# Opening attention's pools with the last projection unit, and moving key tiles and weight measures

## The chip, the cores and the metric

One core of a Trainium2 chip runs the whole kernel. The metric is the device time of one execution in microseconds (us); lower is better. The core has a matrix engine (PE, with its weight loads PEld), three elementwise engines (DVE, ACT and POOL) and SP, which here only issues DMAs. Each engine takes its instructions in the order in which they were written into its queue, and waits at one whose inputs or buffers are not ready.

## The reference

One inference step of a decoder with two layers, for a prompt of 2048 tokens and for 32 tokens of samples (8 sequences of 4). Every matrix product in the kernel is computed from two f16 halves, high and low, in three products.

```python
def even_mixer(h, w_in, b_fox, lb, hgrn_gain, w_out, hgrn_s0, fox_attend):
    proj = h @ w_in
    qa, fa, ia, ga, qb, kb, vb, gb, fb = _split(proj, ...)
    o_a, s_a = gated_linear_chunked(ha(qa), ha(1.0 - f), ha(ia), ha(jnp.log(f)), hgrn_s0)
    ...
    o_b = fox_attend(hb(qb), kb_h, vb_h, log_fb).reshape(bsz, L, B_WIDTH) * jax.nn.silu(gb)
    out = jnp.concatenate([o_a, o_b], axis=-1) @ w_out

def block(args):                                  # of fox_prompt: 128 queries, 4 heads
    logits = einsum('bthd,bshd->bhts', qi, k) * scale + ci[..., None] - c[:, :, None, :]
    logits = jnp.where(t[:, None] >= key_pos[None, :], logits, -jnp.inf)
    p = jax.nn.softmax(logits, axis=-1)
    return jnp.einsum('bhts,bshd->bthd', p, v)
```

`fox_sample` is the same attention for the sample's 32 tokens against 2048 cached tokens per sequence, gathered from pages, plus the new ones. Layer 1 (`odd_mixer`) is a gated linear attention with its own projections. Each layer adds its output to the residual.

## The kernel before, in words

The program has three stages. The **even phase** multiplies the normalized tokens by the input weights of layer 0 in 32 units, 16 for each half of the prompt (`staged`, `dense`): `v0 g0 qf0 qf1 Bq0 Bg0 v1 g1 qf2 qf3 Bq1 Bg1 Bk0 Bv0 Bk1 Bv1`. Unit 31 is `Bv1` of the second half, the last value projection of attention; its products are `pt_Bv110`, `112`, `114` and `116`, which DVE takes out of PSUM into `Bv` and `Bvs`. Beside the units run smaller jobs. `ahead` loads cached keys for the sample's attention (`kp`), turns them on DVE (L1526, four transposes for one entry of `KEYS`) and multiplies them (`ks`); `KEYS` lists the steps, four to a unit, at which this is done. `beside` loads weights of later units and measures their largest values on DVE (L302, four reductions to a weight); `LATER` lists the units in which a load starts, and the measure follows one unit later. A weight's measure is needed only when that weight is split, in a later stage.

The **attention phase** (`phase_fox`) opens its pools when the even phase's have closed, so that it cannot start beside unit 31. It then draws from two generators: `fox_prompt` (for each head h and each group G of 512 queries, four blocks of scores and then the group's values) and `fox_sample`. `until(self.prompt, FOX_P, sample, FOX_S)` draws from whichever is behind by the ratio 270000 to 500000, where each generator yields its own count of ns of PE time, and ends with the sample. Counting the yields gives 233,267 for the prompt and 395,600 for the sample. So the prompt stands at 213,624 when the sample ends, and 19,643 are left.

A score block is a chain: products `s` (PE), maximum `mx` with the bias `cb`/`cm` (DVE, L1412), exponential (ACT, L1420), scale (POOL, L1428). Its values are a second chain: transposes `pt` (PE, L1448), high half `th` (ACT, L1455), low half `tl` (DVE, L1456), products `fo` (PE), result `fy` (DVE, L1471), store (POOL's queue, L1473). The blocks of the first groups are short, those of G=3 long. The PSUM tag `s` has two banks, `t` two, and `kt` two, which the values use as well once the sample is done (`alone`). The sample begins with `past`, which issues a gather and a burst of constants on POOL and goes on to DVE and PE.

The **odd phase** begins with the output projection of layer 0 (`pt_o`). Its first inputs come from `prepare()`: it splits the weight `w_o000` (halves on ACT, DVE L356, POOL L359 and L363) and the first two pieces of attention's output, `yr0000` and `yr000256`, 256 tokens each (ACT, DVE L1854, POOL L1847 and L1851). Before the change `prepare()` is drawn beside what is left of the prompt: `mux(self.prompt, REST_P, prepare(), REST_S)`, L2131. A piece is split in four steps of two input tiles k: k=0 and 4 on ACT (high) and DVE (low); k=2 and 6 (`YPOOL`) are scaled by POOL (L1847), then high on ACT, low on POOL (L1851). Of the weight, parts 0 and 2 go over POOL, 1 and 3 over ACT and DVE. `pt_o0000` needs 24 products for each 128 tokens, three for each k from 0 to 7. The tag `yr` has two buffers; `wr_o000` and `yr0000` take them, and `yr000256` and `yr000512` follow in them.

The schedule is fixed when the program is built. Several scheduler rules (`issue_after`, priorities) move single instructions ahead of their place, so the order on each engine is shown below where it matters.

Of the kernel before, what the change touches and what calls it, by code (L numbers as in the profile page):

```python
# [19 lines left out]
P = 128  # L20
# [18 lines left out]
EWR = 4  # L39
# [10 lines left out]
KEYS = (*range(4 * 13, 4 * 17, 4), *range(4 * 17, 4 * 31, 2))  # L50
LATER = (*range(4, 14), *range(17, 27))
# [4 lines left out]
FOX_P = 270000.0  # L56
LIN3_A = 40000.0
# [66 lines left out]
class Kern:  # L124
# [1221 lines left out]

    def phase_fox(self):
        tc, nc = self.tc, self.nc
        self.fox = ExitStack()
        f1, f0 = (self.fox.enter_context(tc.tile_pool(name=x, bufs=2, reuse_waits="tile")) for x in ("fe", "fx"))  # L1350
        pp1, pp0 = (self.fox.enter_context(tc.tile_pool(name=x, bufs=2, space=PSUM, reuse_waits="tile"))
                    for x in ("fpa", "fpb"))
        if True:
            fx = Pool(f0, {"P": 20},
                      Pool(f1, {"caus": 1, "q2": 3, "k2": 6, "cb": 2, "st1": 12, "cm": 2, "th": 4, "tl": 4, "y": 1, "v2": 6, "sg": 3}))
            pps = Pool(pp0, {"t": 2, "o": 1, "kt": 2}, Pool(pp1, {"s": 2, "sc": 1}))
            caus = fx.tile([P, P], F32, tag="caus", name="caus")
            nc.gpsimd.memset(caus, 0.0)
            nc.gpsimd.affine_select(caus, caus, [[-1, P]], ALU.is_ge, FAR, base=0, channel_multiplier=1)
            with tc.tile_pool(name="fs", bufs=1, side="right", reuse_waits="tile") as s0:  # L1360
                fs = Pool(s0, {"pg": PG, "kt": 2})
                self.prompt = self.fox_prompt(fx, pps, caus)
                drain(until(self.prompt, FOX_P, self.fox_sample(fs, pps), FOX_S))
# [898 lines left out]
```

## Time and profile before

| | |
|---|---|
| time, median of 3 runs (lowest to highest) | 2288.54 us (2284.19 to 2293.45) |
| the profiled execution: time / span | 2291.65 us / 2289.9 us |
| busy share of the span: PE, DVE, ACT, POOL | 96%, 61%, 43%, 32% |
| granted PE clock, mean | 0.99 |
| unit 31 | 887.8 to 911.4 us |
| attention phase | 911.4 to 1239.0 us |

All times inside the trace count from the start of the span. An idle time stands at the instruction that ended it, with the engine, tile and line that released it. PE is busy nearly all the time, so what counts is where it is not, and what it waited for there.

### The profile page before, as it was taken

The page shows a single profiled execution, that of the slowest core. Times are in us where ns is not written, and L with a number is a line of the kernel's source. Part 1 is how long each engine was busy: PE and PEld are TensorE (multiplying, and loading weights), DVE is VectorE, ACT ScalarE, POOL GpSimd, SP SyncE. Part 2 cuts the span into 40 slices and gives each one's busy share as a digit, 9 for nine tenths or more (in the row PEclk, how much of TensorE's full clock was granted, in tenths as well). Part 3 has the DMA queues.
Part 4 walks back from the last instruction along what each step waited for, and adds up shares of the span by engine and source line. Part 5 has one row for each costly group of instructions (what it writes and reads, how often), then busy time and mean ns, then how long its engine had stood idle before and what let it go on. Part 6 is the DMA issues. An engine that isn't in the chain of part 4 may idle for free.

```text
span 2289.9 us, 58071 instructions
## 1 busy us (share of the span) xinstructions
PE 2195.9 (96%) x23316; PEld 1569.0 (69%) x23316; DVE 1400.7 (61%) x3154; ACT 994.3 (43%) x2216; POOL 724.9 (32%) x787
## 2 busy tenths in 40 slices
PE   7999999999999999899999999999999999999998
PEld 5667667774575588455457888677677667567887
DVE  7767677735564466877776454366665655557454
ACT  5434434321221221566667353554644644555243
POOL 2233234100110111544445354154442422232232
PEclk9999999999999999999999999999999999999999
DMA  7444545796575475977735779324325421115554
GB/s 235 144 124 150 160 150 185 233 238 151 159 184 138 118 204 149 280 223 246 223 111 170 260 219 253 101 71 144 92 97 101 120 79 59 54 52 179 171 179 152
DMA packets 361984, 364.02 MB, mean 159 GB/s; under 512 B 108161, under 2 KB 305090, under 8 KB 357490
## 3 DMA queue, kind: packets, MB, share of 16 engines
q1 hardware_dynamic: 359570, 353.69, 52.7%
q0 software_dynamic: 2144, 6.62, 0.8%
q8 instruction: 183, 3.00, 0.6%
q14 instruction: 87, 0.71, 0.1%
HBM read 245.85 MB, written 97.47 MB: 150 GB/s over the span
## 4 chain that ended last, share of the span: by engine, by line
PE 42%; DVE 3%; ACT 2%; DMA 2%; POOL 2%; issue 1%; SPq 0%; POOLq 0%; DVEq 0%; ACTq 0%
PE pt_o L625 4%; PE pt_o L626 4%; PE pt_o L627 4%; PE pt_Cv L625 2%; PE pt_Cv L627 2%; PE pt_Cv L626 2%; PE o_C L909 1%; PE gl_C L756 1%; PE pt L1448 1%; POOL s_C L842 1%; PE py_C L728 1%; ACT L L1420 1%; DMA wr_o<-in_w_out_odd 1%; PE fo L626 0%; PE fo L627 0%
## 5 line engine op out<-in xcount | busy, mean ns | idle before, releaser
L625 PE MATMUL pt_o<-w_o,act 128*128 128x256 f16 x1024 | 279.4, 273 | 1.4 <-ACT sg1C L682 1.4
L626 PE MATMUL pt_o<-w_o,act 128*128 128x256 f16 x1024 | 279.7, 273 | 0.0
L627 PE MATMUL pt_o<-w_o,act 128*128 128x256 f16 x1024 | 279.3, 273 | 0.0
L625 PEld LDWEIGHTS <-act 128*128 128x128 f16 x2304 | 226.1, 98 | 42.3 <-issue 5.3
L626 PEld LDWEIGHTS <-act 128*128 128x128 f16 x2304 | 226.3, 98 | 31.3 <-issue 2.2
L627 PEld LDWEIGHTS <-act 128*128 128x128 f16 x2304 | 226.1, 98 | 31.4 <-issue 2.6
L789 POOL TENSOR_TENSOR kA<-kA,fA 128x512 f32<-128x512 f32 (+1 forms) x56 | 74.2, 1325 | 367.9 <-PE gl_A L756 307.5
L625 PE MATMUL pt_Cv<-w_Cv,act 128*128 128x256 f16 (+1 forms) x512 | 141.5, 276 | 0.9 <-DVE rh L1959 0.8
L627 PE MATMUL pt_Cv<-w_Cv,act 128*128 128x256 f16 (+1 forms) x512 | 141.4, 276 | 0.0
L626 PE MATMUL pt_Cv<-w_Cv,act 128*128 128x256 f16 (+1 forms) x512 | 141.3, 276 | 0.0
L1420 ACT ACTIVATE L<-L,nm,kc 128x512 f32<-128x512 f32 (+3 forms) x160 | 118.2, 741 | 39.4 <-DVE nm L1418 36.1
L1428 POOL TENSOR_SCALAR L<-L,nm 128x512 f32<-128x512 f32 (+3 forms) x160 | 98.2, 629 | 87.4 <-DVE nm L1424 33.7
L789 POOL TENSOR_TENSOR kC<-kC,fC 128x512 f32<-128x512 f32 (+1 forms) x56 | 81.8, 1461 | 136.6 <-PE gl_C L756 93.1
L1455 ACT ACTIVATE th<-pt 128x512 f16<-128x512 f32 (+3 forms) x159 | 80.9, 526 | 74.1 <-PE pt L1448 73.4
L1526 DVE STREAM_TRANSPOSE kt<-kp 128x512 f32<-128x512 f32 x128 | 82.1, 684 | 40.7 <-DMA kp<-in_cache_fox_k 39.7
L1456 DVE TENSOR_TENSOR tl<-pt,th 128x512 f16<-128x512 f32 (+3 forms) x159 | 94.4, 607 | 16.0 <-ACT th L1455 15.0
L1448 PE MATMUL pt<-ident,L 128*128 128x128 f32 x544 | 89.8, 280 | 9.0 <-DVE tl L1456 5.6
L1448 PEld LDWEIGHTS pt<-ident,L 128*128 128x128 f32 x544 | 65.8, 143 | 39.1 <-DVE tl L1456 10.1
L788 DVE TENSOR_TENSOR qC<-qC,fC 128x512 f32<-128x512 f32 (+1 forms) x56 | 72.9, 1302 | 21.1 <-PE gl_C L756 21.1
L1950 ACT ACTIVATE vC<-pt_Cv,kc 128x512 f32<-128x512 f32 (+1 forms) x40 | 23.9, 598 | 134.0 <-PE pt_Cv L627 134.0
L625 PE MATMUL pt_Bv<-w_Bv,act 128*128 128x260 f16 (+1 forms) x256 | 70.8, 277 | 3.9 <-DVE Bvs L1070 3.9
L363 POOL TENSOR_TENSOR w_o<-wr_o,w_o 128x512 f16<-128x512 f32 x32 | 46.5, 1467 | 79.1 <-ACT w_o L362 55.2
(959 smaller groups left out, 6460.4 us busy)
## 6 DMA issues: line engine op xcount, KB each, us to landing
kp<-in_cache_fox_k SPq DMA_DIRECT2D x128, 256.0 KB, 4.9
pgcache_fox_v<-in_cache_fox_v SPq DMA_DIRECT2D x128, 256.0 KB, 4.1
yr<-yT SPq DMA_DIRECT2D x16, 1024.0 KB, 7.0
x1d<-xo SPq DMA_DIRECT2D x44, 256.0 KB, 4.1
wr_o<-in_w_out_even SPq DMA_DIRECT2D x32, 256.0 KB, 5.5
xo<-in_x_prompt SPq DMA_DIRECT2D x32, 256.0 KB, 4.5
wr_Cv<-in_w_in_odd SPq DMA_DIRECT2D x32, 256.0 KB, 3.4
x1r<-x1d SPq DMA_DIRECT2D x16, 512.0 KB, 4.5
```

The source lines that it names most:

```text
L363: nc.gpsimd.tensor_tensor(lo, r, hi, ALU.subtract)
L625: nc.tensor.matmul(ps, lh[0], rh[0], start=first, stop=False)
L626: nc.tensor.matmul(ps, lh[0], rh[1], start=False, stop=False)
L627: return nc.tensor.matmul(ps, lh[1], rh[0], start=False, stop=last)
L788: nc.vector.tensor_tensor(xv[:, :, 1], xv[:, :, 1], t0.to_broadcast([P, nb, w]), ALU.mult)
L789: nc.gpsimd.tensor_tensor(kv[:, :, 0], kv[:, :, 0], t1.to_broadcast([P, nb, w]), ALU.mult)
L1420: self.last_exp = nc.scalar.activation(lt[:, :w], lt[:, :w], AF.Exp, bias=nm[:, 0:1], scale=ib, accum_out=nm[:, 2 + j : 3 + j])
L1428: nc.gpsimd.tensor_scalar(lt[:, :w], lt[:, :w], nm[:, 1:2], 2.0**14, ALU.mult, ALU.mult)
L1448: nc.tensor.transpose(pt[:, w : w + P], rows[b][s // 4][0][:, (s % 4) * P : (s % 4 + 1) * P], self.ident)
L1455: nc.scalar.activation(th[:, a:w], pt[:, a:w], AF.Copy),
L1456: nc.vector.tensor_tensor(tl[:, a:w], pt[:, a:w], th[:, a:w], ALU.subtract)))
L1526: return self.nc.vector.transpose(kt[:, :, 32 * x : 32 * x + 32], t[:, x].rearrange("p (a e) -> p a e", e=32))
```

## The change

The pools of attention are opened when all of the even phase's pools but the weights, the activations and three PSUM banks have closed, and `until(self.prompt, FOX_A, last, 21120.0)` draws 14000 of the prompt among unit 31's products. `phase_fox` opens the remaining PSUM pool (`kt`, `sc`) and goes on from there. `KEYS` puts two entries into units 13 and 14 in place of one, and ends one unit earlier, so that no key tiles are turned beside unit 31. `LATER` leaves out units 12 and 13 and adds 27 and 28. The sample yields 18000 more after POOL's constants, before DVE and PE use them, so that its count is 413,600 in place of 395,600. In the odd phase nothing is edited.

```diff
-KEYS = (*range(4 * 13, 4 * 17, 4), *range(4 * 17, 4 * 31, 2))
-LATER = (*range(4, 14), *range(17, 27))
+KEYS = (*range(4 * 13, 4 * 15, 2), 4 * 15, 4 * 16, *range(4 * 17, 4 * 30, 2))
+LATER = (*range(4, 12), *range(17, 29))
+FOX_A = 14000.0
...
         with pool("act", side="right") as ap, pool("w", side="right") as w0, pool("wl", side="right") as wp1, \
-                pool("wk") as wp0, pool("nrm") as n0, pool("stt") as sp, pool("ps", space=PSUM) as pp0:
-            wpool = self.wpool = Pool(w0, {"w": 3, "wr": EWR, "rm": 3, "pow": 3, "lr": 1})
+                pool("pj", space=PSUM, side="right") as pp1:
+            inner = ExitStack()
+            wk, wp0, n0, sp = (inner.enter_context(pool(x)) for x in ("wr", "wk", "nrm", "stt"))
+            pp0 = inner.enter_context(pool("ps", space=PSUM))
+            wpool = self.wpool = Pool(w0, {"w": 3}, Pool(wk, {"wr": EWR, "rm": 3, "pow": 3, "lr": 1}))
...
-            pps = Pool(pp0, {"pj": 3, "gr": 2, "st": 1, "o": 2})
+            pps = Pool(pp0, {"gr": 2, "st": 1, "o": 2}, Pool(pp1, {"pj": 3}))
...
                 last = dense(15, 16)
-            drain(last)
-            for t in range(4 * 32, 4 * 32 + 2):
-                self.ahead(wpool, pps, t)
+            inner.close()
+            self.fox_open()
+            drain(until(self.prompt, FOX_A, last, 21120.0))
...
+    def fox_open(self):
+        nc = self.nc
+        self.fox = ExitStack()
+        f1, f0 = self.fox_pool("fe"), self.fox_pool("fx")
...
+        self.more_banks = Pool(None, {"kt": 2, "sc": 1})
+        self.fox_banks = Pool(self.fox_pool("fpa", space=PSUM), {"t": 2, "o": 1, "s": 2}, self.more_banks)
...
+        self.prompt = self.fox_prompt(fx, self.fox_banks, caus)
+
     def phase_fox(self):
...
+        self.more_banks.pool = self.fox_pool("fpb", space=PSUM)
+        with self.tc.tile_pool(name="fs", bufs=1, side="right", reuse_waits="tile") as s0:
+            fs = Pool(s0, {"pg": PG, "kt": 2})
+            drain(until(self.prompt, FOX_P, self.fox_sample(fs, self.fox_banks), FOX_S))
...
+            yield 18000
             tots = one([P, NH], "tots")
             nc.vector.reduce_sum(tots, lfp.rearrange("p s h -> p h s"), axis=mybir.AxisListType.X)
```

Line numbers after the change are 1 higher up to the even phase, and 8 or 9 higher from attention on (L1448 becomes L1456, L1851 becomes L1860).

PE, at the border of unit 31 and attention. Tiles `s000`, `s010` are scores of head 0, group 0, blocks 0 and 1; `pt0000` is the first transposed block; `pt_Bv112` to `116` belong to unit 31. Before:

```order
L627 MATMUL pt_Bv116_12572<-w_Bv11_11533,act_121 128x256
...
L625 MATMUL s000_12672<-k2_00_12660,q2_00_12659 128x128
...
L625 MATMUL s010_12695<-k2_00_12660,q2_00_12659 128x256
...
L625 MATMUL s020_12710<-k2_00_12660,q2_00_12659 128x384
...
L625 MATMUL s030_12725<-k2_00_12660,q2_00_12659 128x512
...
L1448 MATMUL pt0000_12770<-ident_58,L000_12676 128x128
```

After:

```order
L626 MATMUL pt_Bv112_12627<-w_Bv11_11658,act_127 128x256
...
L626 MATMUL s000_12434<-k2_00_12422,q2_00_12421 128x128
...
L626 MATMUL s010_12516<-k2_00_12422,q2_00_12421 128x256
...
L627 MATMUL pt_Bv112_12627<-w_Bv11_11658,act_127 128x256
...
L626 MATMUL s020_12531<-k2_00_12422,q2_00_12421 128x384
...
L626 MATMUL s030_12546<-k2_00_12422,q2_00_12421 128x512
...
L1456 MATMUL pt0000_12591<-ident_58,L000_12438 128x128
...
L626 MATMUL s040_12562<-k2_00_12422,q2_01_12504 128x512
...
L627 MATMUL pt_Bv116_12897<-w_Bv11_11658,act_127 128x256
...
L626 MATMUL fo00_12558<-th0000_12596,v2_00_12423 128x512
```

The last product of unit 31 stood ahead of the first score. Now the scores of group 0, most of group 1's and the first values (`fo00`) stand among the products of `pt_Bv112`, `114` and `116`.

SP's DMA queue at the same place. `q2`, `k2`, `v2` and `cb` are attention's loads, `vd1` stores of unit 31's values, `cbd` the store of the bias that `cb0` reads back. Before:

```order
L1325 DMA cbd_80<-cmask_11954 64x128
L1084 DMA vd1_75<-Bvs110_12403 128x2x512
L1084 DMA vd1_75<-Bvs112_12484 128x2x512
L1564 DMA scd_85<-scs15_12429 128x128
L1084 DMA vd1_75<-Bvs114_12545 128x2x512
L1384 DMA q2_00_12659<-qd_71 128x2x512
L1386 DMA_TRANSPOSE k2_00_12660<-kd0_72 128x2x512
L1377 DMA cb0_12664<-cbd_80 128x512
```

After:

```order
L1329 DMA cbd_80<-cmask_12092 64x128
L1392 DMA q2_00_12421<-qd_71 128x2x512
L1394 DMA_TRANSPOSE k2_00_12422<-kd0_72 128x2x512
L1385 DMA cb0_12426<-cbd_80 128x512
L1396 DMA v2_00_12423<-vd0_74 128x4x256
...
L1085 DMA vd1_75<-Bvs110_12490 128x2x512
```

The loads stood behind three stores of `vd1`, each of which waits for a product of unit 31. Now they follow `cbd` at once.

POOL at the end of the prompt. `L315.` are scales of the last score block, `fy320`, `fy330` and `fy332` the last three results, `ys` the sample's; `w_o000`, `yr0000` and `yr000256` are `prepare()`'s. Before:

```order
L359 TENSOR_SCALAR wr_o000_17999<-wr_o000_17999,kc_67 128x512 x2
...
L363 TENSOR_TENSOR w_o000_18006<-wr_o000_17999,w_o000_18006 128x512
L1847 TENSOR_SCALAR yr0000_18004<-yr0000_18004,kc_67 128x512 x2
L363 TENSOR_TENSOR w_o000_18006<-wr_o000_17999,w_o000_18006 128x512
L1428 TENSOR_SCALAR L3150_17968<-L3150_17968,nm315_18032 128x512
...
L1851 TENSOR_TENSOR act_17992<-yr0000_18004,act_17992 128x2x256
...
L1851 TENSOR_TENSOR act_17992<-yr0000_18004,act_17992 128x2x256
L1847 TENSOR_SCALAR yr000256_18126<-yr000256_18126,kc_67 128x512 x2
L1851 TENSOR_TENSOR act_17992<-yr000256_18126,act_17992 128x2x256 x2
L1473 DMA yT0_81<-fy330_18179 128x256
...
L1473 DMA yT0_81<-fy332_18311 128x256
```

After:

```order
L1436 TENSOR_SCALAR L3153_17839<-L3153_17839,nm315_17888 128x512
L1481 DMA yT0_81<-fy320_17915 128x512
L1777 DMA yT0_81<-ys_13859 128x32 x4
L1481 DMA yT0_81<-fy330_18069 128x256
L360 TENSOR_SCALAR wr_o000_18280<-wr_o000_18280,kc_67 128x512 x2
L1481 DMA yT0_81<-fy332_18241 128x256
L364 TENSOR_TENSOR w_o000_18287<-wr_o000_18280,w_o000_18287 128x512 x2
L1856 TENSOR_SCALAR yr0000_18285<-yr0000_18285,kc_67 128x512 x2
L1860 TENSOR_TENSOR act_18279<-yr0000_18285,act_18279 128x2x256 x2
L1856 TENSOR_SCALAR yr000256_18300<-yr000256_18300,kc_67 128x512 x2
L1860 TENSOR_TENSOR act_18279<-yr000256_18300,act_18279 128x2x256 x2
```

Before, all of `prepare()`'s POOL work stood ahead of the store of `fy332`, the prompt's last. Now only the scale of `wr_o000` does; the rest stands behind that store. DVE and ACT have `prepare()`'s work behind the prompt's last `tl` and `th` in the same way.

## Rows read from the trace of the kernel before

**Rows 1.** The page's part 1, busy time and share of each engine.

```profile
PE 2195.9 (96%) x23316; PEld 1569.0 (69%) x23316; DVE 1400.7 (61%) x3154; ACT 994.3 (43%) x2216; POOL 724.9 (32%) x787
```

**Rows 2.** Windows at attention's start: length, then each engine's busy time, PE's clock.

```profile
core 0: us, PE busy (x) PEld busy (x) DVE busy (x) ACT busy (x) POOL busy (x), PEclk, DMA share, GB/s
900.00:910.00 10.00, 10.00 (x116) 8.68 (x115) 5.93 (x11) 1.89 (x4) 1.97 (x4) 1.00 0.32 111
911.40:932.00 20.60, 12.90 (x65) 6.14 (x65) 14.56 (x65) 9.92 (x26) 10.13 (x23) 0.83 1.05 294
932.00:950.00 18.00, 12.75 (x69) 6.89 (x70) 12.82 (x49) 11.62 (x30) 14.58 (x33) 1.00 1.07 326
950.00:960.00 10.00, 9.97 (x86) 6.50 (x85) 9.44 (x37) 6.58 (x18) 4.32 (x7) 1.00 0.78 259
```

**Rows 3.** PE's waits, 905 to 932 us: total us, times, longest.

```profile
PE s L625 <- DVE mx L1412: 3.5, 4, 2.6
PE s L625 <- DVE Bvs L1070: 3.0, 1, 3.0
PE pt L1448 <- POOL L L1428: 1.0, 2, 0.6
```

**Rows 4.** Windows with a lowered clock, columns as above.

```profile
915.00:922.00 7.00, 4.05 (x12) 1.17 (x9) 3.88 (x22) 2.42 (x7) 2.79 (x7) 0.51 1.08 304
1215.50:1225.50 10.00, 8.05 (x32) 5.01 (x33) 6.92 (x16) 6.81 (x16) 7.41 (x8) 0.50 0.36 107
```

**Rows 5.** Timeline of SP's DMA issues around 900 us: start, length, line.

```profile
892.19 0.51 SPq L1325 DMA_DIRECT2D cbd<-cmask  x1
908.63 1.73 SPq L1384 DMA_DIRECT2D q<-qd  x1
910.46 1.28 SPq L1386 DMA_TRANSPOSE k<-kd  x1
```

**Rows 6.** DMA issues, 900 to 950 us: count, size, median us to landing.

```profile
cb<-cbd SPq DMA_DIRECT2D x7, 256.0 KB, 5.1
k<-kd SPq DMA_TRANSPOSE x6, 6.1
```

**Rows 7.** PE's waits, 390 to 430 us.

```profile
PE pt_Bv L625 <- DVE Bvs L1070: 3.9, 3, 1.7
```

**Rows 8.** Timeline of DVE around 410 us, idle before in brackets.

```profile
409.37 0.69 DVE L302 TENSOR_REDUCE rm_Cqk<-lr_Cqk 128x1 f32<-128x512 f32 x1 [1.04 <-DMA lr_Cqk<-in_w_in_odd]
412.99 0.69 DVE L302 TENSOR_REDUCE rm_Cqk<-lr_Cqk 128x1 f32<-128x512 f32 x1 [0.86 <-DMA lr_Cqk<-in_w_in_odd]
```

**Rows 9.** The page's part 5: key tiles turned on DVE.

```profile
L1526 DVE STREAM_TRANSPOSE kt<-kp 128x512 f32<-128x512 f32 x128 | 82.1, 684 | 40.7 <-DMA kp<-in_cache_fox_k 39.7
```

**Rows 10.** Windows at the prompt's end and behind the border.

```profile
1205.00:1225.00 20.00, 15.17 (x74) 8.87 (x73) 15.91 (x42) 15.31 (x34) 17.41 (x19) 0.76 0.18 54
1240.00:1249.50 9.50, 9.50 (x90) 8.49 (x88) 1.25 (x2) 6.16 (x10) 1.71 (x2) 1.00 1.02 341
```

**Rows 11.** Timeline of DVE, 1213 to 1240 us.

```profile
1213.49 1.73 DVE L356 SCALAR_TENSOR_TENSOR w_o<-wr_o,kc,w_o 128x512 f16<-128x512 f32 x1
1216.02 1.84 DVE L1854 SCALAR_TENSOR_TENSOR act<-yr,kc,act 128x512 f16<-128x512 f32 x2
1239.18 0.48 DVE L1471 SCALAR_TENSOR_TENSOR fy<-fo,kc,fsg 128x256 f32<-128x256 f32 x1 [0.94 <-PE fo L627]
```

**Rows 12.** Timeline of POOL, 1227 to 1240 us.

```profile
1227.42 3.69 POOL L1847 TENSOR_SCALAR yr<-yr,kc 128x512 f32<-128x512 f32 x2
1231.09 2.27 POOL L1851 TENSOR_TENSOR act<-yr,act 128x512 f16<-128x512 f32 x2
1239.96 0.55 POOL L1473 DMA_DIRECT2D yT<-fy  x1 [1.01 <-DVE sam_o L665]
```

**Rows 13.** Line L363, whole trace: shortest, median, longest ns.

```profile
L363 POOL TENSOR_TENSOR w_o<-wr_o,w_o x32: 1149/1253/3247, 1213.5 to 2220.3; 128x512 f16<-128x512 f32 x32
```

**Rows 14.** Tile yr, 1175 to 1300 us: from issue to landing.

```profile
DMA to landing us min/median/max: 2.6/6.3/11.6
```

More of the change, by code (lines that the diff above doesn't have):

```diff
@@ L1345, in log_sigmoid @@
         nc.vector.scalar_tensor_tensor(zz, q, -2.0, zz, ALU.mult, ALU.add)
-    def phase_fox(self):
[L1348 to L1363, printed above, removed]
@@ new lines, in fox_pool @@
+    def fox_pool(self, name, **kw):
+        return self.fox.enter_context(self.tc.tile_pool(name=name, bufs=2, reuse_waits="tile", **kw))
+    def fox_open(self):
+        nc = self.nc
+        self.fox = ExitStack()
+        f1, f0 = self.fox_pool("fe"), self.fox_pool("fx")
+        fx = Pool(f0, {"P": 20},
+                  Pool(f1, {"caus": 1, "q2": 3, "k2": 6, "cb": 2, "st1": 12, "cm": 2, "th": 4, "tl": 4, "y": 1, "v2": 6, "sg": 3}))
+        self.more_banks = Pool(None, {"kt": 2, "sc": 1})
+        self.fox_banks = Pool(self.fox_pool("fpa", space=PSUM), {"t": 2, "o": 1, "s": 2}, self.more_banks)
+        caus = fx.tile([P, P], F32, tag="caus", name="caus")
+        nc.gpsimd.memset(caus, 0.0)
+        nc.gpsimd.affine_select(caus, caus, [[-1, P]], ALU.is_ge, FAR, base=0, channel_multiplier=1)
+        self.prompt = self.fox_prompt(fx, self.fox_banks, caus)
```

## The prediction

> **What bounds the kernel now.** I read the page's busy shares first: PE is busy for 96% of the span [rows 1], so 94 us of idle PE is nearly all that a change of order can win, besides stretches at a lowered clock. Then I read the windows around the places that the change touches. Attention's start stands out. In 900 to 910 us, inside unit 31, PE is busy 10.00 of 10 us while DVE is busy 5.93, ACT 1.89 and POOL 1.97; from 911.4 to 932 us PE is busy only 12.90 of 20.60 us, from 932 to 950 us 12.75 of 18.00, and from 950 us it is full again [rows 2]. So 7.70 us are idle in the first stretch and 5.25 us in the second. The waits name the causes: 3.0 us once on DVE's `Bvs` and 3.5 us on the maxima `mx` [rows 3]. The first has a wrong label. DMA issues show that `q` is issued only at 908.63 us and `k` at 910.46 us, while the bias store `cbd` ahead of them went at 892.19 us [rows 5]; the first score waits for `k`, whose loads take a median of 6.1 us in this stretch [rows 6]. The second is a chain: PE, DVE, ACT and POOL pass one short block on, and nothing else is there for PE. Both happen because attention begins when unit 31 has ended. The idle time also costs clock: the granted clock is 0.51 from 915 to 922 us, the lower level of 1.2 GHz, with PE busy for 4.05 us of it [rows 4]; at the upper level the same work takes half, so 2.0 us more are lost.
>
> **Part 1, the early start.** The chance is to hide what lies before 932 us beside a unit that leaves the other engines idle. The listing shows how far the prompt gets among unit 31's products: all scores of group 0, most of group 1's and group 0's values, which is what PE does until about 932 us before. The chance is 7.70 + 2.0 = 9.7 us. Two things come off. First, `q2_00` now follows `cbd`: with `cbd` at 892.2 us, `q` 1.7 us and `k` 1.3 us long at issue [rows 5], `k2_00` is issued at about 894.5 us and landed by 898 to 900.5 us if 3.5 us (estimate, from the idle 3.0 us after the issue at 910.46 us) to 6.1 us pass. PE reaches `s000` after 91 products of unit 31, 887.8 + 91 x 0.106 = 897.5 us, at 0.106 us a product (90 in 9.50 us [rows 10]). That leaves 0.5 to 3 us, of which I take 1, since DMAs are less busy there (share 0.32 at 900 us against 1.05 [rows 2]). Second, the added yield of 18000 keeps the sample back for 0.54 x 18000 = 9.7 us of prompt work, in which the prompt is alone. Alone it lost 5.25 us in 18 us [rows 2], 0.29 us per us, so up to 2.8 us; in 950 to 960 us, with groups that are longer, nearly nothing. I take 1. The 5.25 us after 932 us I leave as they are: they are `mx` chains of group 2 and POOL's constants (POOL busy 14.58 of 18 us), and the change does not take either away. Part 1 gives 9.7 - 1 - 1 = **7.7 us**, bounds 2 and 14 (with all 5.25 us gone).
>
> **Part 2, key tiles and measures.** From 390 to 430 us, PE waits three times, 3.9 us in all, for `Bvs` in unit 13 [rows 7]. Just ahead of it DVE measures `Cqk2`: four reductions of 0.69 us and waits of 1.04 and 0.86 us for their loads [rows 8], 4.6 us in all with DVE waiting at the head of its queue. `LATER` without units 12 and 13 takes these away from here, more than the 3.9 us by which PE is late. They return as 2.7 us of DVE work (the 4 reductions) around units 27 to 29; two entries of `KEYS` in unit 13 and 14 bring eight transposes of 0.684 us [rows 9] where four were, 2.7 us more of DVE. Unit 31 loses its own. Where PE has no wait in these units now, DVE has room for them; in unit 13 it may keep a part of the 3.9 us late. I take **2.5 us** (3.9 less half of 2.7), bounds 0 and 4.
>
> **Part 3, the prompt's end.** Before, `prepare()` stands among the last blocks, and it shows: from 1205 to 1225 us PE is busy 15.17 of 20 us [rows 10], with DVE's `w_o` and `act` splits of 1.73 and 1.84 us ahead of the `tl` that PE waits for [rows 11]. Then the clock is 0.50 for 10 us with 8.05 us of work [rows 4], 4.0 us lost. Together 4.8 + 4.0 = 8.8 us. After the change, the prompt is 14000 ahead and the sample counts 413,600, so the prompt would stand at 14,000 + 0.54 x 413,600 = 237,344 when the sample ends. It has only 233,267. It runs out first, and the listing shows `prepare()` behind it. The splits no longer disturb the last blocks, but the exponentials of the last block still stand in one chain, the values find only two banks (`alone` is false), and the sample's copies now fall among them; I take 5.5 of the 8.8 us back.
>
> The price is at the border. Take T as the end of the last `fo` product. On POOL, the store of `fy332` waits for DVE's `fy` (0.48 us [rows 11]) and takes 0.55 us to issue [rows 12]. Behind it stand two `w_o` low halves of 1.25 us (the median [rows 13]), two scales of `yr0000` (3.69 us) and its two low halves (2.27 us) [rows 12]: T + 0.48 + 0.55 + 2.5 + 3.69 + 2.27 = T + 9.5 us. The products of `pt_o0000` need the first of those low halves at k=2 and the second at k=6. By T + 9.5 us PE can have done 18 products, 18 x 0.106 = 1.9 us. So PE stands 7.6 us where it went on without a gap before. Then `yr000256`: its buffer is that of `wr_o000`, free at about T + 4 us, and a load takes 6.3 us to landing [rows 14]; with 0.7 us on ACT the first product of `pt_o0002`, two products on from there, waits till about T + 11.3 us: 1.6 us more. `yr000512` has the buffer of `yr0000`, free at T + 9.5 us, landed at T + 16 us, some 1.6 us late again. Together 10.8 us, and I add 2 us for the lowered clock behind such a gap, as after 915 us [rows 4]. Border: **-12.8 us**, bounds -5 (if half of it is covered) and -20 (below). Part 3 is 5.5 - 12.8 = -7.3 us.
>
> On POOL's term, a row shows a wide spread: the same `w_o` low half takes 1.149 to 3.247 us [rows 13], and DVE's split at 1213.49 us took 1.73 us, that at 1216.02 us 0.92 us for the same amount [rows 11]. The Trainium skill (GPSIMD Engine Reference, Key points) says why that may be: POOL shares its SBUF interfaces with DVE, and they contend when the DVE instruction has two SBUF inputs, as these splits have. By that rule the border is a bad place, since the change sets DVE's four splits and POOL's six operations side by side; by it the `w_o` term would be 6.5 us in place of 2.5 us and the sum 4 us worse.
>
> **Sum.** 7.7 + 2.5 + 5.5 - 12.8 = +2.9 us won. The profiled execution took 2291.65 us, which becomes 2288.8 us. It lies 3.1 us above the median of the runs, 2288.54 us; from that I predict 2285.6 us. One measurement of this kernel tells from no change what is over 0.5%, 11.4 us.
>
> **Rivals.**
> A, the start gains all and the tail is clean: ahead by 14 us, the prompt meets the sample with long groups, as in 950 to 960 us, so the 5.25 us go too, and all 8.8 us of the tail. 7.70 + 5.25 + 2.0 - 1 + 2.5 + 8.8 - 12.8 = 12.5 us, 2276.0 us. For it: every wait named there is one of short blocks. Against it: DVE was busy 12.82 of 18 us there, and POOL's burst remains.
> B, the border decides, slower: POOL's two halves at 3.25 us (+4.0 us) and the load of `yr000256` at its longest, 11.6 us in place of 6.3 [rows 13, 14]. PE stands 11.6 us to k=6, then to T + 4 + 11.6 + 0.7 = T + 16.3 us, 2.6 us more, and again for `yr000512`, 3 us; with 2.8 us of clock it is 20 us. With a start of 5 us, 1 us from part 2 and 2 us back at the tail, 12 us are lost: 2300.5 us. It decides from a border of 7.7 + 2.5 + 5.5 = 15.7 us on. Against it: the median of that operation is 1.25 us, and 6.3 us that of the loads.
> C, the change only moves the stall: loads and `mx` chains then hold PE inside unit 31, since its queue is in order. `k` at 6.1 us gives 3 us at `s000`, `cb` at 5.1 us [rows 6] another 2 us at `s020`, so that part 1 gives 3 us; 3 + 2.5 + 5.5 - 12.8 = -1.8 us, 2290.3 us.
>
> **How the numbers follow.** Forecast 0.45, A 0.25, B 0.15, C 0.15. A lies just over the bound: two thirds of it are faster by over 0.5%, and one fifth of the forecast's spread, 0.26 in all. Half of B and a tenth of the forecast and C are slower by over 0.5%: 0.13. The rest, 0.61, is within. The range reaches from A with part 2 at its upper bound and the border 3 us cheaper, 2271 us, to just short of B, 2299 us; the forecast's own is 2278 to 2293 us.
>
> **What would show it.** Right: PE with no idle time of over 1 us in unit 31, less than 6 us idle from its end to 40 us later, and a clock of 1.00 there; no wait for `Bvs` in unit 13; at the border an idle of 6 to 9 us before `pt_o0000`, released by POOL's `act` or `yr`, and one of 1 to 2 us released by the load of `yr`. Wrong: a border with under 4 us of idle (A), one over 15 us (B), or idle of over 4 us on `s` inside unit 31 (C).

## Result: 0.42% slower

The changed kernel takes 2297.27 us (median of 18 runs, 2290.00 to 2309.15), the kernel before 2289.01 us beside it (18 runs, 2284.19 to 2299.98). The ratio is 1.0042, 95% interval 1.0030 to 1.0053: 9.6 us lost, where 2.9 us gained were forecast. The time lies inside the predicted range, the sign is wrong.

The page of the changed kernel shows busy times that answer to [rows 1]:

```profile
span 2295.4 us, 58071 instructions
PE 2196.7 (96%) x23316; PEld 1569.3 (68%) x23316; DVE 1401.7 (61%) x3154; ACT 994.9 (43%) x2216; POOL 725.9 (32%) x787
```

PE works as long as before, to 0.8 us. So the loss is idle PE, and the question is where. The profiled execution took 2297.09 us, 5.4 us more than that of before (2291.65 us), so the two profiles show only a part of the 9.6 us. Where a stage starts later than before, the time was lost ahead of it. The starts are those of the first product of each stage in the two timelines (in us; negative is earlier):

| start of | before | after | lost or won since the row above |
|---|---|---|---|
| unit 13 | 392.67 | -4.00 | 4.0 won |
| unit 14 | 430.87 | -4.37 | |
| unit 15 | 454.14 | -1.83 | 2.5 lost |
| unit 16 | 477.44 | +1.30 | 3.1 lost |
| unit 18 | 523.38 | +8.00 | 6.7 lost |
| unit 31, the last even one | 887.78 | +8.89 | 0.9 lost |
| out-projection (`pt_o0000`) | 1238.97 | -0.91 | 9.8 won: unit 31, attention and its tail |
| odd layer's first `Cv` | 1410.79 | +8.26 | 9.2 lost: the border |
| end | | +5.5 | 2.7 won |

Attention and the border together come out near the forecast: one gives about what the other takes. In these two profiles the loss is in the even phase, where 2.5 us were to be gained. PE's waits from 390 to 520 us in the changed kernel (columns: total us, times, longest; [rows 7] has before's, to 430 us):

```profile
PE pt_Bk L626 <- DVE Bvs L1071: 7.4, 1, 7.4
PE ks L1579 <- DVE kt L1534: 6.7, 3, 4.1
PE pt_Av L626 <- DVE Bvs L1071: 0.7, 1, 0.7
```

The waits of `pt_Bv` in unit 13 are gone, as forecast. In their place PE stands once for 7.4 us at unit 14's start, and for 6.7 us at the products of the key tiles. The DMA issues from 400 to 432 us say why. First the kernel before, then the changed one (count, KB each, median us to landing; the last line is for the `vd` stores alone):

```profile
kp<-in_cache_fox_k SPq DMA_DIRECT2D x4, 256.0 KB, 4.1
vd<-Bvs SPq DMA_DIRECT2D x3, 256.0 KB, 3.6
DMA to landing us min/median/max: 2.2/3.6/5.3
```

```profile
kp<-in_cache_fox_k SPq DMA_DIRECT2D x8, 256.0 KB, 5.9
vd<-Bvs SPq DMA_DIRECT2D x4, 256.0 KB, 6.9
DMA to landing us min/median/max: 3.5/6.9/10.0
```

A key tile is four loads of 256 KB, 1 MB. With the second tile of unit 13 in the same stretch, the stores of the unit's values, `vd<-Bvs`, land after a median of 6.9 us in place of 3.6. A buffer of `Bvs` comes free only when its store has landed. The timelines of DVE and SP show one such wait (start, length, operation, idle time before it):

```profile
424.73 0.48 DVE L1064 TENSOR_SCALAR Bv<-pt_Bv,kc 128x256 f32<-128x256 f32 x1 [6.13 <-DMA vd<-Bvs]
```

```profile
411.31 2.79 SPq L1530 DMA_DIRECT2D kp<-in_cache_fox_k  x4
...
414.66 0.39 SPq L1085 DMA_DIRECT2D vd<-Bvs  x1
```

This store is the one that took 10.0 us. It was issued behind the second tile's four loads and a 1 MB store of a weight (`wd`), which the kernel before has there too. DVE stands 6.13 us for it, then empties unit 13's PSUM, and unit 14's first product waits for that. The table hides it: without this wait unit 14 would start some 11.8 us early (an estimate, 4.37 and 7.4; it is 10.4 us in e7, which has no second tile there), not 4.4. Later the loads of the next tiles are late themselves. SP, DVE and PE around 510 us:

```profile
498.70 1.88 SPq L1530 DMA_DIRECT2D kp<-in_cache_fox_k  x4
...
505.23 1.82 SPq L1530 DMA_DIRECT2D kp<-in_cache_fox_k  x4
```

```profile
509.37 2.49 DVE L1534 STREAM_TRANSPOSE kt<-kp 128x512 f32<-128x512 f32 x4 [22.59 <-DMA kp<-in_cache_fox_k]
```

```profile
511.92 1.93 PE L1579 MATMUL ks<-kt,qz 128*32 128x128 f32 x32 [4.05 <-DVE kt L1534]
513.78 0.61 PE L626 MATMUL pf_Ag<-act,w_Ag 128*128 128x512 f16 x1
...
517.99 0.38 PE L627 MATMUL pf_Ag<-act,w_Ag 128*128 128x512 f16 x1
```

The four loads issued from 498.70 us on land after 7.0 to 9.0 us (in e9, below, they were issued from 497.09 us on and landed after 4.7 to 6.8). DVE turns the tile as soon as the last has landed, but that is late (509.37 us; 504.27 us in the kernel before), and PE stands 4.05 us at the head of its queue. After that gap the products run at 0.61 us each where 0.38 us is had at 517.99 us: the granted clock is 0.50 from 512 to 518 us, the lower level of 1.2 GHz.

At attention's start the windows of the changed kernel answer to [rows 2] (unit 31, then the next 20.6 and 18 us; same columns):

```profile
896.70:926.80 30.10, 29.64 (x246) 23.60 (x246) 18.43 (x66) 10.57 (x28) 10.33 (x19) 1.00 0.90 222
926.80:947.40 20.60, 16.53 (x94) 8.75 (x91) 18.55 (x70) 14.40 (x36) 12.65 (x27) 1.00 1.06 335
947.40:965.40 18.00, 14.71 (x92) 9.62 (x92) 12.92 (x41) 11.16 (x31) 13.46 (x26) 1.00 0.82 276
```

Unit 31 carries the prompt's opening groups with 0.46 us idle, and the clock stays at 1.00; 4.07 and 3.29 us are idle behind it, where before it was 7.70 and 5.25 us. The prompt's tail, against [rows 10]:

```profile
1215.00:1225.00 10.00, 8.64 (x74) 6.60 (x74) 6.69 (x13) 4.53 (x11) 3.22 (x5) 1.00 0.07 28
1225.00:1235.00 10.00, 9.38 (x85) 8.21 (x84) 8.87 (x26) 4.42 (x8) 5.79 (x7) 1.00 0.07 21
```

18.02 of 20 us are busy, at full clock. The 20 us of [rows 10] (15.17 us busy) end some 13 us earlier, as seen from the prompt's end. From 1185 us to the prompt's end, 3.43 us are idle in place of 6.15, and the clock, 0.50 for 10 us before [rows 4], stays at 1.00. The border follows, as timelines of PE, DVE and POOL:

```profile
1238.06 0.28 PE L626 MATMUL pt_o<-w_o,act 128*128 128x256 f16 x1 [1.73 <-ACT act L1862]
1238.99 0.27 PE L627 MATMUL pt_o<-w_o,act 128*128 128x256 f16 x1 [0.65 <-POOL w_o L364]
1242.85 0.40 PE L628 MATMUL pt_o<-w_o,act 128*128 128x256 f16 x1 [3.58 <-DVE act L1863]
```

```profile
1236.37 0.48 DVE L1479 SCALAR_TENSOR_TENSOR fy<-fo,kc,fsg 128x256 f32<-128x256 f32 x1 [0.64 <-PE fo L628]
1236.77 4.48 DVE L357 SCALAR_TENSOR_TENSOR w_o<-wr_o,kc,w_o 128x512 f16<-128x512 f32 x2
1241.17 4.73 DVE L1863 SCALAR_TENSOR_TENSOR act<-yr,kc,act 128x512 f16<-128x512 f32 x2
```

```profile
1237.76 2.28 POOL L364 TENSOR_TENSOR w_o<-wr_o,w_o 128x512 f16<-128x512 f32 x2
1240.01 3.11 POOL L1856 TENSOR_SCALAR yr<-yr,kc 128x512 f32<-128x512 f32 x2
1243.09 2.25 POOL L1860 TENSOR_TENSOR act<-yr,act 128x512 f16<-128x512 f32 x2
```

The three gaps are 5.96 us, the largest released by DVE's split of `act`, not by POOL. Behind them the products come 0.21 us apart until 1248.3 us and 0.11 us apart from there on; the granted clock is 0.73 from 1236.3 to 1248 us. The rows give DVE's four splits in pairs; one by one they take 0.74 and 3.82 us (`w_o`) and 1.62 and 3.19 us (`act`). In [rows 11] the `w_o` split took 1.73 us and the two of `act` 0.74 and 1.18 us, although POOL was at work beside these as well.

### The profile page after: what moved, and what is told of

It reads as the page before. It is cut to its first block, busy times and chain, and to the rows that moved or that the text cites. A ratio compares the mean times of both kernels' runs of the same rounds, so it can differ in the third digit from the quotient of the medians.

```text
span 2295.4 us, 58071 instructions
## 1 busy us (share of the span) xinstructions
PE 2196.7 (96%) x23316; PEld 1569.3 (68%) x23316; DVE 1401.7 (61%) x3154; ACT 994.9 (43%) x2216; POOL 725.9 (32%) x787
## 4 chain that ended last, share of the span: by engine, by line
PE 46%; DVE 4%; DMA 3%; POOL 2%; ACT 2%; issue 2%; SPq 1%; POOLq 0%; DVEq 0%; ACTq 0%
PE pt_o L627 4%; PE pt_o L626 4%; PE pt_o L628 4%; PE pt L1456 2%; PE pt_Cv L626 2%; PE pt_Cv L628 2%; PE pt_Cv L627 2%; PE pv L1759 1%; PE o_C L910 1%; PE gl_C L757 1%; PE fo L626 1%; PE fo L627 1%; PE fo L628 1%; PE s L626 1%; PE s L628 1%
## 5 line engine op out<-in xcount | busy, mean ns | idle before, releaser
L1456 PE MATMUL pt<-ident,L 128*128 128x128 f32 x544 | 89.8, 279 | 3.7 <-DVE tl L1464 2.0
L1456 PEld LDWEIGHTS pt<-ident,L 128*128 128x128 f32 x544 | 65.5, 143 | 33.0 <-DVE tl L1464 8.8
L626 PE MATMUL pt_Bk<-w_Bk,act 128*128 128x256 f16 x256 | 70.5, 275 | 7.4 <-DVE Bvs L1071 7.4
L626 PE MATMUL pt_Av<-w_Ai,act 128*128 128x256 f16 x256 | 70.9, 277 | 1.3 <-DVE Bvs L1071 0.7
```

What stands on the lines that cost most here:

```text
L626: nc.tensor.matmul(ps, lh[0], rh[0], start=first, stop=False)
L1456: nc.tensor.transpose(pt[:, w : w + P], rows[b][s // 4][0][:, (s % 4) * P : (s % 4 + 1) * P], self.ident)
```

## The experiments

Each was timed in five rounds beside the kernel before, on the same chip as that. The first theory was that the key tiles cost it: two tiles moved from units 30 and 31 into units 13 and 14, into a stretch full of transfers. Its rivals: the moved measures (`LATER`), the border, or the early start itself. "New `KEYS`" and "new `LATER`" are the lists of the change.

**e1 and e2: one list each, in the kernel before.**

```diff
 e1, from before:
-KEYS = (*range(4 * 13, 4 * 17, 4), *range(4 * 17, 4 * 31, 2))
+KEYS = (*range(4 * 13, 4 * 15, 2), 4 * 15, 4 * 16, *range(4 * 17, 4 * 30, 2))
 e2, from before:
-LATER = (*range(4, 14), *range(17, 27))
+LATER = (*range(4, 12), *range(17, 29))
```

> The kernel before with the new KEYS alone (two key tiles in units 13 and 14, single in 15 and 16, none beside unit 31). Theory 1 (the second key tile loses the time: its 1 MB load stands in the DMA queue ahead of unit 13's store of Bvs, and the loads of the next two tiles come late): slower than before by 6 to 10 us, about 2297 us, with PE waits of several us at the end of unit 13 and on ks in units 15 to 17. Theory 2 (the new place of the weight buffers, wr in an inner pool, delays the loads) and theory 3 (the moved measures of LATER do it): no change, 2289 us within 2 us.

> The kernel before with the new LATER alone (no fetches in units 12 and 13, two more in 27 and 28). Theory 1: 2 to 4 us faster than before, about 2286 us, since the 3.9 us of waits for Bvs in unit 13 go and nothing takes their place. Theory 3 (LATER is what loses the time): 5 us or more slower than before. Theory 2: no change.

e1: 2297.72 us, ratio 1.0032 (1.0020 to 1.0045), 7.3 us lost. e2: 2285.91 us, 0.9976 (0.9963 to 0.9989), 5.5 us won. The two halves of part 2 have opposite signs, and the half that was priced at a loss of 1.35 us of DVE work costs 7.3 us. In e2's profile unit 14 starts 9.7 us early and PE's waits from 390 to 520 us are small:

```profile
PE pt_Bk L625 <- DVE Bvs L1070: 1.0, 1, 1.0
PE pt_Av L625 <- DVE Bvs L1070: 0.7, 1, 0.7
PE ks L1571 <- DVE kt L1526: 0.6, 1, 0.6
```

**e3 and e4: other places for the tiles, other end of the prompt.**

```diff
 e3, from after:
-KEYS = (*range(4 * 13, 4 * 15, 2), 4 * 15, 4 * 16, *range(4 * 17, 4 * 30, 2))
+KEYS = (48, 50, *range(4 * 13, 4 * 17, 4), *range(4 * 17, 4 * 30, 2))
 e4, from after:
-FOX_S = 500000.0
+FOX_S = 560000.0
```

> The changed kernel with another KEYS: two tiles in unit 12, one each in units 13 to 16, then two per unit up to unit 29, so that unit 31 stays free of key work and units 13 and 14 have one tile each as before. Theory 1: 6 to 10 us faster than the changed kernel, 2288 us, about the time of before or below it. Theories 2 and 3: no change from the changed kernel, 2297 us.

> The changed kernel with FOX_S = 560000 in place of 500000, so that the prompt stands at 14,000 + 0.482 x 413,600 = 213,400 when the sample ends, as before the change, and prepare() finds about 20,000 of it to stand beside. Theory A (the border's 9 us come from prepare() being uncovered): the idle PE at the border goes, the disturbed last blocks of before return with up to 8.8 us, so 1 to 5 us faster than the changed kernel, 2292 to 2296 us. Theory B (the border's waits come from the loads and POOL's queue, whatever is drawn beside): no change at the border, 2297 us.

e3 (both extra tiles in unit 12): 2299.05 us, 1.0036 (1.0022 to 1.0050). By the times no better than after. Its unit 14 starts 1.8 us late, where that of after starts 4.4 us early. e4 (the sample lasts longer, so that `prepare()` is covered again): 2298.73 us, 1.0039 (1.0026 to 1.0053). The border's cost falls from 9.2 to 5.7 us, and the stretch from unit 31 to the border wins 6.0 us in place of 9.8: a part of the cost moves into the last blocks, as PE's waits from 1210 to 1265 us show:

```profile
PE fo L626 <- ACT th L1463: 4.8, 2, 3.1
PE pt_o L626 <- ACT w_o L363: 2.9, 1, 2.9
PE fo L627 <- DVE tl L1464: 1.8, 3, 0.7
PE pt_o L627 <- POOL w_o L364: 1.0, 1, 1.0
```

**e5: new `KEYS` in the kernel before, the two extra tiles without their loads.** Their tiles are filled with zeros by POOL, so the sample's key products of these two are left out of the result; all of DVE's and PE's work on them stays.

```diff
 e5, from e1:
                 for x in range(4):
+                    if n in (1, 3):
+                        nc.gpsimd.memset(kp[:, x], 0.0)
+                        continue
                     self.page_load(kp, "cache_fox_k", regs[x], x)
```

> The kernel before with the new KEYS (measured at +7 us), but the second key tiles of units 13 and 14 are filled with zeros on POOL in place of their 1 MB loads; it leaves out these two loads, and everything else of the tiles (turning on DVE, products) stays. Theory load (the second tile's loads crowd the DMA queue there): back to 2289 us within 2 us. Theory DVE (the four more transposes of 0.68 us per unit ahead of the evictions that PE waits for lose the time): stays near 2297 us.

2292.54 us, 1.0001 (0.9988 to 1.0014), against 1.0032 for e1: without 2 MB of loads, the 7.3 us are gone. The stores of `Bvs`, 400 to 432 us, e1 and then e5:

```profile
kp<-in_cache_fox_k SPq DMA_DIRECT2D x8, 256.0 KB, 4.8
vd<-Bvs SPq DMA_DIRECT2D x3, 256.0 KB, 8.1
```

```profile
kp<-in_cache_fox_k SPq DMA_DIRECT2D x4, 256.0 KB, 4.9
vd<-Bvs SPq DMA_DIRECT2D x3, 256.0 KB, 2.6
```

The key loads land as fast in the one as in the other. The medians of the stores are not of the same stores: in e1 only the second of the unit's stores has a landing on record, 8.1 us; the second one in e5 took 5.0 us (5.3 in the kernel before). What costs the time is transfers, not work: that the times show. How much of the 7.3 us goes through this store they do not. e1's profile, of its fastest execution (e5's is of its slowest), has PE waiting 2.3 us at unit 14's start and 2.3 us for key tiles.

**e6: after, with no early start.**

```diff
-FOX_S = 500000.0
+FOX_S = 470000.0
-FOX_A = 14000.0
+FOX_A = 0.0
```

> The changed kernel without the early start: FOX_A = 0, so that the prompt begins behind unit 31 as before, and FOX_S = 470000, so that the prompt runs out at the same place of the sample as in the changed kernel and the border to the next layer stays as it is there. Theory 1 (the early start gains 7 to 10 us): 7 to 10 us slower than the changed kernel, about 2305 us. Rival (the early start gains nothing, its waits only move): as the changed kernel, 2297 us.

2303.74 us, 1.0050 (1.0031 to 1.0069), 1.8 us over after by the ratios (11.4 against 9.6 us), which the intervals do not separate. In the profile the stretch from unit 31 to the out-projection wins 2.8 us here, 9.8 us in after: 7.0 us for the start by this pair, the size of part 1 (7.7 us). Other kernels with the new `KEYS` and no early start scatter in this stretch: 5.2 us won in e1, 5.6 in e9, 1.8 lost in e13, all below. So single profiles give the start some 4 to 12 us.

**e7: after, with two key tiles less.** The last two tiles are not turned at all, so their part of the sample is left out of the result.

```diff
-KEYS = (*range(4 * 13, 4 * 15, 2), 4 * 15, 4 * 16, *range(4 * 17, 4 * 30, 2))
+KEYS = (*range(4 * 13, 4 * 17, 4), *range(4 * 17, 4 * 30, 2))
...
             nc.sync.dma_start(self.scd[:, j * P : (j + 1) * P], self.scs)
+            if j == 14:
+                nc.sync.dma_start(self.scd[:, 15 * P :], self.scs)
```

> The changed kernel with one key tile each in units 13 to 16 and two per unit in 17 to 29: 30 of the 32 tiles; it leaves out the last two tiles of the cached keys. Theory 1 (the two tiles that came from unit 30 cost about 7 us wherever they stand in units 12 to 14): 2290 us. Rival (the new place of the weight buffers or the moved measures lose the time): 2296 us or more.

2284.93 us, 0.9976 (0.9962 to 0.9989). In the changed kernel two key tiles in units 13 and 14 are worth 15 us (0.9976 against 1.0042); their own work on PE is about 2 us of that (the 32 products of one take 1.08 us in e9's trace). Unit 14 starts 10.4 us early, attention wins 9.7 us and the border loses 8.7 us, as in after: the rest of the change is as it was.

**e8: other units left out of `LATER`.**

```diff
 from before:
-LATER = (*range(4, 14), *range(17, 27))
+LATER = (*range(4, 12), *range(17, 24), *range(26, 31))
```

> The kernel before with LATER in units 4 to 11, 17 to 23 and 26 to 30, so that no fetch falls in units 24 and 25, where the new LATER alone showed DVE waiting 5.4 us for a key tile behind a 1 MB fetch and PE 4.9 us behind DVE. Theory (that collision takes back 4 to 5 us): 2 to 5 us faster than the new LATER alone, 2281 to 2284 us. Rival (it only moves to another unit): 2286 us.

2286.58 us, 0.9977 (0.9965 to 0.9989), the same as e2. So these two do not tell where the fetches should go. In e2's profile the moved fetches make a wait of 4.9 us (`gl_A` on DVE's `qA`, 640 to 760 us), which e8's does not have, but e8 has one of 2.9 us (`ks` on `scs`) that e2's lacks and before's shows too.

**e9: both lists in the kernel before.**

```diff
 from before: KEYS as in e1, LATER as in e2
```

> The kernel before with the new KEYS and the new LATER, and nothing else of the change. Alone they measured +7 us and -5.5 us. Theory sum (they add): +2 us, 2292 us. Theory bound (without the measures PE runs ahead in unit 13 until it meets the store of Bvs that the second tile's load delays, so LATER's gain is lost and the key tiles' price shows in full): +8 to +10 us, 2299 us, that is the whole loss of the change, with the early start and the border behind it cancelling each other.

2291.78 us, 1.0010 (0.9994 to 1.0026), 2.3 us lost; e1 and e2 add up to 1.8. So the two lists do not share one bound. With the new `LATER` the tiles cost 7.8 us here (1.0010 against 0.9976 in e2), about as without it, and 15 us in the changed kernel (e7). Beyond the lists, 7.3 us of after's loss (9.6 less 2.3) come with the moved pools, the early start and the yield. Without the tiles these cost nothing that the times show: e7 has the ratio of e2, 0.9976, though it also spares the two tiles' own work. Yet e9 has after's order, instruction for instruction on each engine, up to the last even unit. Its waits from 390 to 520 us:

```profile
PE pt_Bk L625 <- DVE Bvs L1070: 7.4, 1, 7.4
PE ks L1571 <- DVE kt L1526: 2.7, 2, 2.0
```

The same 7.4 us in unit 14, but 4.0 us less on the key tiles. Unit 18 starts 1.25 us late in e9, 8.00 us in after.

**e10, e11 and e12: after, with the pressure lowered.**

```diff
 e10, from after:
-LATER = (*range(4, 12), *range(17, 29))
+LATER = (*range(4, 11), *range(17, 30))
 e11, from e10:
-FOX_S = 500000.0
+FOX_S = 530000.0
 e12, from after:
-KEYS = (*range(4 * 13, 4 * 15, 2), 4 * 15, 4 * 16, *range(4 * 17, 4 * 30, 2))
+KEYS = (*range(4 * 12, 4 * 16, 4), *range(4 * 16, 4 * 30, 2))
```

> The changed kernel with LATER in units 4 to 10 and 17 to 29, so that one more 1 MB fetch leaves the DMA queue ahead of unit 13, where the second key tile's load and the store of Bvs stand. Theory load: the 7.4 us wait at the end of unit 13 shrinks, 3 to 8 us faster than the changed kernel, 2289 to 2294 us. Rival (the wait there belongs to the tile's own 1 MB alone): as the changed kernel, 2297 us.

> The same with FOX_S = 530000, so that some 9,000 of the prompt are left beside prepare() when the sample ends. Theory: half of the border's 9 us come back and less than that is lost in the prompt's last blocks, 2 to 4 us faster than with 500000. Rival (as with 560000, what the border wins the last blocks lose): no difference.

> The changed kernel with key tiles single in units 12 to 15 and two per unit from unit 16 on, 32 in all. Theory load (a second tile costs where the DMA queue carries stores that PE waits for, and unit 16 has fewer of them than unit 13): 4 to 8 us faster than the changed kernel, 2289 to 2293 us. Rival (the two tiles cost about the same wherever they stand, as they did in unit 12): 2297 us.

e10 (one unit's measures less ahead of unit 13): 2289.11 us, 1.0002 (0.9989 to 1.0016). e11: 2287.63 us, 0.9992 (0.9978 to 1.0005), not told from e10. e12 (one tile a unit from unit 12, two from 16): 2290.04 us, 1.0007 (0.9995 to 1.0020). The fetch of one unit's measures, or the place of the double tiles, takes back 8 to 9 of the 9.6 us. The wait at unit 14 falls to 1.4 us in e10, 390 to 520 us:

```profile
PE ks L1579 <- DVE kt L1534: 4.7, 3, 2.2
PE pt_Bv L626 <- DVE Bvs L1071: 2.2, 1, 2.2
PE pt_Bk L626 <- DVE Bvs L1071: 1.4, 1, 1.4
```

**e13, e14 and e15: e10 taken apart.** The theory that was left: the start and the border together are a net loss.

```diff
 e13, from before: KEYS as in e1, LATER as in e10 (pools, start and yield as before)
 e14, from before: LATER as in e10
 e15, from e10:
-            yield 18000
```

> The kernel before with the new KEYS and with LATER in units 4 to 10 and 17 to 29; no early start, the odd phase's prepare() beside the prompt as before. The same two lists with the early start measured 2289 us. Theory net loss (with the key tiles off unit 31, attention's loads are early anyway; the early start then adds 4 us and its uncovered prepare() costs 9): 3 to 6 us faster than with the early start, about 2285 us. Rival (early start and border cancel): 2289 us.

> The kernel before with LATER in units 4 to 10 and 17 to 29 and nothing else; the old KEYS with one tile each in units 13 to 16 and two beside units 30 and 31's work. Theory (the even phase gains 5 to 6 us as with the new LATER, and unit 13 has no second tile to lose it to): 2283 to 2286 us. Rival (the two tiles are better off unit 31 when the DMA queue has room in unit 13): slower than the kernel with the new KEYS.

> The changed kernel with LATER in units 4 to 10 and 17 to 29 (2289 us) and without the added yield of 18000, so that the sample begins its products earlier and some 5,600 of the prompt are left beside prepare(). Theory: the border's cost falls by 1 to 3 us and PE waits 1 to 3 us more for POOL's constants and the gather at the start; no change within 2 us, 2289 us. Rival (the yield is what costs at the border): 4 us or more faster.

e13: 2295.49 us, 1.0016 (1.0002 to 1.0029). e14: 2290.09 us, 0.9992 (0.9978 to 1.0006), not the gain of e2 that was expected. e15: 2290.71 us, 0.9993 (0.9982 to 1.0003). From e14 to e13 the tiles cost 5.5 us again (0.0024; the intervals just overlap); from e13 to e10 the pools, the start and the border together give 3.2 us (0.0014; the intervals overlap). So with these lists they are no net loss; with the lists of after they were one, of 7.3 us (e9). The yield shows no effect.

**e16: after, with the pools moved and nothing else of part 1.**

```diff
-FOX_A = 14000.0
+FOX_A = 0.0
...
-            yield 18000
```

> The changed kernel with FOX_A = 0 and without the added yield: new KEYS, new LATER and the new pools, but only the first score's products are drawn ahead of unit 31 and prepare() finds 19,600 of the prompt to stand beside, as before. Against the new KEYS and LATER alone (2291.8 us, +2.3 us over before) it has the pools' other places in memory, and the even phase's order is the same to the row. Theory start (what the change loses beyond KEYS and LATER lies in the early start and the border): 2290 to 2293 us. Theory place (the buffers' other places make the same loads of unit 13 to 17 land later): 2296 us or more, with PE waits of 4 us on ks near 510 us.

2304.88 us, 1.0056 (1.0037 to 1.0075), 12.8 us lost. Unit 31 starts 10.8 us late, 5.0 us in e9, with the even phase in the same order. Windows over the stretch of late key tiles, 460 to 515 us, in e9, after and e16 in this order (columns as in [rows 2]):

```profile
460.00:515.00 55.00, 52.15 (x531) 40.48 (x524) 19.11 (x35) 11.07 (x24) 0.00 (x0) 1.00 1.05 247
```

```profile
460.00:515.00 55.00, 47.54 (x475) 37.94 (x475) 18.89 (x34) 10.51 (x23) 0.00 (x0) 0.96 1.03 222
```

```profile
460.00:515.00 55.00, 49.15 (x512) 39.20 (x509) 19.17 (x34) 10.49 (x23) 0.00 (x0) 0.97 1.07 236
```

The DMA engines are as busy (1.03 to 1.07) and move less: 222 and 236 GB/s against 247. It is tempting to blame the pools' places, since only the addresses of the buffers are known to differ up to there. But after, e4, e6 and e16 have the same even phase in the same pools, and their profiles differ as much among themselves (starts against the kernel before, in us):

| | waits for key tiles (`ks`), 390 to 520 us | unit 18 | unit 31 | GB/s, 460 to 515 us |
|---|---|---|---|---|
| e9 | 2.7 | +1.3 | +5.0 | 247 |
| after | 6.7 | +8.0 | +8.9 | 222 |
| e4 | 4.0 | +2.3 | +8.3 | 231 |
| e6 | 4.9 | +3.4 | +6.6 | 226 |
| e16 | 5.8 | +8.7 | +10.8 | 236 |

With the lists of e10 there is no such difference: unit 31 starts at +0.2 us in e13 (old pools, 227 GB/s) and at -0.5 us in e10 (moved pools, 219 GB/s). Without the early start e16 also pays at attention, one wait of 5.2 us for POOL between 900 and 970 us:

```profile
PE pt L1456 <- POOL L L1436: 5.2, 1, 5.2
```

So that the places slow the transfers is not shown.

## Why the prediction was wrong

**The step that failed is part 2**, "eight transposes of 0.684 us [rows 9] where four were, 2.7 us more of DVE". A key tile was priced by what DVE does with it. Its load of 1 MB was left out, though [rows 8] and [rows 9] show DVE waiting for loads already. Measured, new `KEYS` costs 7.3 us by itself (e1), nothing without its loads (e5, in the kernel before) and 15 us in the changed kernel (e7). The other half, `LATER`, won 5.5 us (e2; its interval, 2.5 to 8.5 us, holds the 3.9 that were said to be on offer). Part 2 was +2.5 us with bounds 0 and 4; both lists together are -2.3 us (e9; 1.4 won to 6.0 lost), and the even phase of after loses 8.9 us in its profile. The sum also took the parts as independent, and that failed too: the tiles cost twice as much in the changed kernel as by themselves. "No wait for `Bvs` in unit 13" came true for the unit's own products, while the wait came back, larger, at unit 14.

**Part 1 was right in mechanism and near in size.** No idle time in unit 31, clock 1.00, `q` and `k` directly behind `cbd`. Of the test "less than 6 us idle from its end to 40 us later", 7.4 us were found in 38.6 us. From unit 31 to the out-projection 9.8 us are won in after, where parts 1 and 3 without the border said 13.2; 2.3 us of it are only moved, since unit 31's key products now stand in units 13 and 14 (unit 31 takes 21.4 us in e1, 23.7 us in before). The start alone is 7.0 us by one pair of profiles (after against e6) and 4.3 us by another (after against e9); by the times it is not told from zero in e6.

**Part 3's tail was right**: the last blocks keep the upper clock and wait 2.7 us less (3.43 in place of 6.15). Whether `prepare()` is better kept out of them than covered by them no run tells: e4 is as fast as after.

**The border was near in size, with another last releaser.** Predicted 12.8 us, measured 9.2 us (8.7 us in e7). I counted POOL's chain to T + 9.5 us; it ended at 1245.34 us, T + 9.0 us with T = 1236.3, the end of the last `fo` product. But PE stood for DVE's `act`, behind two `w_o` splits, which I had left out of the sum. In place of one idle of 6 to 9 us there were three, of 1.73, 0.65 and 3.58 us, released by ACT, POOL and DVE; the lowered clock behind them, put at 2 us, accounts for most of the rest. DVE's splits were 0.74 to 3.82 us, against 0.74 to 1.73 us before, while POOL's `w_o` halves took 1.16 and 1.18 us (the median of [rows 13] is 1.25). The Trainium skill (GPSIMD Engine Reference, Key points) says that POOL and a DVE instruction with two SBUF inputs contend. The trace agrees in part: POOL was at work beside the long splits, but beside the short ones of before too. By that rule I had put the cost on POOL's side, and it fell on DVE's. The loads of `yr`, said to cost 1.6 us twice, cost PE 0.25 us: ACT waits for one, and PE for ACT.

**The rivals.** A needed a cheap border, B a dear one, C a stall in unit 31. None came as described: the time of 2297 us is near B's 2300.5, and inside the stated range, by luck: the cause is another. B's mechanism is wrong, since the border stayed at 9.2 us, under the 15.7 us from which it decides. No rival had a late transfer in the even phase, though the changed lists put one there.

**What stays open.** Of after's 9.6 us, 2.3 us are the two lists by themselves (e9). The other 7.3 us appear when the pools, the start and the yield are added to these lists; added to those of e10 they gave 3.2 us instead (e13 to e10), and without the tiles nothing (e7 against e2). Why they double the tiles' price is open. The profiles of e9 and after do not put it in one place: in after the even phase is 3.9 us longer, attention and the border together give 4.5 us less, and 3.2 us come back behind them. Single profiled executions also scatter: e1's took 2289.95 us, its median is 2297.72. The verdicts above therefore rest on ratios, the stages on what repeats in several profiles (attention -7.6 to -10 us and border +8.7 to +9.2 us in after, e3, e7, e10, e12).

**The better version** is e2, the new `LATER` alone: 2285.91 us, 0.9976 of before. e8 is its equal.

## What to carry to other kernels

Price a moved step by its transfers first: list what it loads, and look at which store or load must land in that stretch for a buffer to come free. An order that is moved to make room at one place (here two tiles, so that pools could open earlier) must be paid for at the place that takes it. That place is judged by when the transfers that free its buffers land, not by its engines' idle time; nor did its DMA share tell it here (400 to 430 us: 0.80 before, 0.87 in after, 0.88 in e7, which is faster than before). Where an edit has two lists or two halves, one run for each shows cancelling effects which their sum hides.

## What was unexpected in the hardware

- The second of unit 13's stores of 256 KB landed after 10.0 us (after), 10.8 us (e9) and 8.1 us (e1) with 1 MB of loads more in the stretch, and after 5.3 us (before), 5.0 us (e5) and 4.3 us (e2, e7) without them. The key loads themselves took a median of 5.9 (after), 4.8 (e1), 4.1 (before) and 4.9 us (e5).
- `DMA_TRANSPOSE act<-xhl` holds SP's queue for 1.81 to 5.35 us at one issue in the kernel before and for 2.07 to 5.21 us in after (eight issues each, 440 to 520 us).
- DVE's `SCALAR_TENSOR_TENSOR` of 128x512 took 0.74 to 3.82 us beside POOL at the border, 0.74 to 1.73 us beside POOL before, and 0.75 us with POOL idle (1251.00 us in the kernel before); POOL's own halves did not lengthen at the border.
- The same order of instructions from the same pools ran with 222, 226, 231 and 236 GB/s between 460 and 515 us in four profiles (after, e6, e4, e16), at a DMA share of 1.03 to 1.07.
